# Token rows stored feature block by feature block, and eight expert loads named early

## The chip, the cores and the metric

One core of a Trainium2 chip runs the whole kernel. The number that counts is the device time of one execution, in microseconds (us), from the first to the last instruction plus a small rest around it; the median of several runs is given. Five engines work side by side: TensorE (PE, with its weight loads shown apart as PEld), VectorE (DVE), ScalarE (ACT), GpSimd (POOL) and SyncE (SP), which here issues the DMA transfers.

## The reference, cut to what matters

Two layers of a model work on 256 tokens of 1024 features. The change lies at the border between the Mamba mixer of layer 2 and the mixture of experts that follows it:

```python
def moe_swiglu(h, w_router, w_gate, w_up, w_down):
    t = h.reshape(bsz * seq, d)
    logits = (t @ w_router).astype(jnp.float32)
    top_vals, top_idx = lax.top_k(logits, TOP_K)          # 2 of 8
    top_w = jax.nn.softmax(top_vals, axis=-1)
    gates = jnp.sum(jax.nn.one_hot(top_idx, N_EXPERTS) * top_w[..., None], axis=1)
    out = jnp.zeros_like(t)
    for e in range(N_EXPERTS):
        out = out + gates[:, e:e+1] * swiglu(t, w_gate[e], w_up[e], w_down[e])
```

Each expert has three float32 matrices of 1024 x 2816 (gate, up) and 2816 x 1024 (down), 34.6 MB together.

## The kernel before, in words

**Stages.** Attention, a dense feed-forward, the Mamba mixer and the experts follow each other. The expert stage is more than half of the time: eight experts' weights stream from HBM, each as 33 loads of 1 MB (11 gate, 11 up, 11 down). Line 133 issues the gate and up loads (`load_flat`), line 139 the down loads (`load_rows`), all on SP's queue. They land in tiles named `raw`: eight in one pool, two more in a second pool that opens with the expert stage. `raw()` goes round these ten by the counter `turn`; a load waits until the tile that it will overwrite has been read.

**Experts by rank.** Every expert computes only its own tokens. Experts are sorted by their number of tokens; expert 0 is put first, as rank 0. Ranks 0, 5, 6 and 7 take up to 64 tokens (class `Small`: the weights go to TensorE as they are, lines 1382 and 1401), ranks 1 to 4 up to 128 (class `Expert`: every weight tile is first split into a high and a low part by ACT and DVE at line 159, then multiplied three times, lines 1290 and 1335). The order is rank 0, then 1, 5, then 2, 6, then 3, 4, then 7. These brackets are groups; a group's tokens are fetched together.

**Fetching tokens.** `halves_of` writes the normalised token rows as two tiles, `xt_hi` and `xt_lo` (high and low parts; tokens on the partitions, 1024 features along the row), from four PSUM banks: four ACT instructions (line 1065) and four DVE instructions (line 1066). `gather` then makes, for each of 8 feature blocks `cc`, one PSUM tile by four matmuls (line 1199): a slice of `xt_hi` or `xt_lo` of 128 tokens x 128 features is loaded as weights, and the 0/1 selection tile `psel` streams through (128 columns for one expert, 256 for two). A block `cc` holds the features p*8 + cc, p = 0 to 127, so the slice takes every eighth float of a row. This order fits the weights, whose row p*8 + cc lies on partition p. There are 32 such matmuls in a group and 160 in all. The first group's run before rank 0 starts. Those of the next group are placed by a table of ticks into the down phase of the last expert before it: in ranks 0, 5 and 6 (256 columns each), and in rank 4 (128 columns).

**What sets the order.** The instructions stand on each engine in an order that a scheduler works out at build time from the program; the order in the source is not always kept. `early` holds gate loads of rank 0 that are named inside the last `ssm_out` of the Mamba stage, and `stream` takes them from there. `rankc` (line 1041, 12 KB of constants) and `fn_row` (line 1432, the last norm's gain) are the small loads of the expert stage.

Of the kernel before, what the change touches and what calls it, by code (L numbers as in the profile page):

```python
# [12 lines left out]
F32R = mybir.dt.float32r  # L13
I32 = mybir.dt.int32
U32 = mybir.dt.uint32
AF = mybir.ActivationFunctionType
# [4 lines left out]
P = 128  # L21
S = 256
D = 1024
DC = D // P
# [56 lines left out]
def body(ctx: ExitStack, tc, x, c, positions, ada_w, ada_b, norm_g,  # L81
# [5 lines left out]
    V, A, PE, G, SP = nc.vector, nc.scalar, nc.tensor, nc.gpsimd, nc.sync  # L87
# [10 lines left out]
    def scoped(ectx, name, bufs=1, side="right"):  # L98
        return ectx.enter_context(tc.tile_pool(name=name, bufs=bufs, side=side, reuse_waits="tile"))
# [8 lines left out]
    def pt(tag):  # L108
        pool, tag, n = banks[tag]
        return pool.tile([P, 512], F32, tag=tag, name=tag, bufs=n)  # L110

    extra, turn, halved = [], [0], []

    def raw(n):

        pool = rawp
        if extra:
            pool = rawp if turn[0] < 8 else extra[0]
            turn[0] = (turn[0] + 1) % (8 + NMORE)
        t = pool.tile([P, 2048], F32, tag="raw", name="raw")  # L120
        return t[:, :n]
# [8 lines left out]
    def load_flat(ap, t):  # L130

        d = raw(FLAT)
        SP.dma_start(d, ap.rearrange("(p j) n -> p (j n)", p=P)[:, t * FLAT:(t + 1) * FLAT])
        return d
# [250 lines left out]
    rtok = per.tile([P, 2], F32, name="rtok")  # L385
# [3 lines left out]
    with ExitStack() as lctx:  # L389
# [36 lines left out]
        for q in range(4):  # L426
            ps = pt("mm")
            for i in range(4):
                cc, j = 2 * q + i // 2, i % 2
# [109 lines left out]
        for t in range(8):  # L539
            ps = pt("mm")  # L540
# [3 lines left out]
        for j in range(2):  # L544
            for nh in range(2):
                ps = pt("mm")
# [65 lines left out]
        for half in range(2):  # L612
            w = load8(mla_w_out[0, :, half * 512:(half + 1) * 512])
            for m in range(2):
                ps = pt("mm")
# [77 lines left out]
    early = []  # L693
    with ExitStack() as lctx:
# [36 lines left out]
        ps, psb0 = pt("in"), pt("y")  # L731
# [10 lines left out]
        xb, e, z, w = (four[:, i, :, :] for i in range(4))  # L742
        q = e
# [60 lines left out]
        m = decay_tiles()  # L804
# [113 lines left out]
        for g in range(SG):  # L918
# [31 lines left out]
            m = m2  # L950
# [31 lines left out]
        pst = {}  # L982
# [26 lines left out]

        def then(m):  # L1010
            if m == 2:
                early.append(load_flat(moe_w_gate[0, 0], 0))
            if m:
                finish(m - 1)
            if m == 5:
                logits(0)
            if m == 6:
                token_rows(0)
            if m == 7:
                logits(2)  # L1020
                token_rows(2)
                token_rows(4)
# [13 lines left out]


    extra.append(scoped(ctx, "rawm", NMORE, "left"))
    ep = scoped(ctx, "moe", 1, "left")
    rankc = ep.tile([P, 3, NE], F32, name="rankc")  # L1040
    SP.dma_start(rankc, consts[:, C_KEY:C_EIGHTH].rearrange("p (z e) -> p z e", z=3))
    x_tok = ep.tile([P, 2, D], F32, name="x_tok")
    xt_hi = ep.tile([P, 2, D], F32R, name="xt_hi")
    xt_lo = ep.tile([P, 2, D], F32R, name="xt_lo")

    top = ep.tile([P, 2, 8], F32, name="top")
    tix = ep.tile([P, 2, 8], U32, name="tix")
# [13 lines left out]

    def halves_of(q, j):

        sl, ps = slice(q * 512, (q + 1) * 512), pst[q, j]
        held = A.activation(xt_hi[:, j, sl], ps, AF.Copy, scale=rtok[:, j:j + 1])
        V.scalar_tensor_tensor(xt_lo[:, j, sl], ps, rtok[:, j:j + 1], xt_hi[:, j, sl],
                               op0=ALU.mult, op1=ALU.subtract)
        return held
    with ExitStack() as cctx:
# [4 lines left out]
    ps = pt("y")  # L1074
# [32 lines left out]
    with ExitStack() as cctx:  # L1107
        cctx.enter_context(tc.issue_after(last.ins))
        for j in range(2):
            held = halves_of(1, j)  # L1110
# [81 lines left out]
    def gather(xs, sel2, cc, first=False):  # L1192


        m = len(xs) * P
        ps = pt("a")
        for i in range(4):
            j, src = i // 2, (xt_hi, xt_lo)[i % 2]
            PE.matmul(ps[:, :m], src[:, j, :].rearrange("t (p c) -> t c p", c=DC)[:, cc, :], sel2[:, j, :, :],  # L1199
                      start=(i == 0), stop=(i == 3))  # L1200

        def empty():
            g, sh = gain8[:, 0, cc:cc + 1], gain8[:, 1, cc:cc + 1]
            big = [i for i, x in enumerate(xs) if len(x) == 2]
            for i, x in enumerate(xs):
                if len(x) == 1:
                    A.activation(x[0][:, cc, :], ps[:, i * P:i * P + FEW], AF.Identity, bias=sh, scale=g)
            if not big:
                return
            n = P * (1 + big[-1])  # L1210
            tt = ew.tile([P, 2 * P], F32, tag="gt", name="gt")
            if first:
                V.tensor_scalar(tt[:, :n], ps[:, :n], g, sh, op0=ALU.mult, op1=ALU.add)
            else:
                A.activation(tt[:, :n], ps[:, :n], AF.Identity, bias=sh, scale=g)
            for i in big:
                split(xs[i][0][:, cc, :], xs[i][1][:, cc, :], tt[:, i * P:(i + 1) * P])
        return empty
# [14 lines left out]
    class Expert:  # L1233
# [32 lines left out]
        def stream(self, which):  # L1266

            for t in range(DC * DFF // FLAT):
                w = early.pop() if early else load_flat(self.w[which], t)
                for h in range(2):  # L1270
                    feed(lambda f=t * FLAT + h * HALF, ws=self.take(w[:, h * HALF:(h + 1) * HALF]):
                         self.columns(which, f, ws))
# [167 lines left out]
    for g, i in seq:  # L1440
# [4 lines left out]
        if g:  # L1445
            which = nc.values_load(tid[0:1, rank:rank + 1], engines=[mybir.EngineType.SP], min_val=0, max_val=NE - 1)
# [165 lines left out]
```

## Time and profile before

| | us |
|---|---|
| median of 3 runs (1308.05 to 1312.42) | 1309.12 |
| the profiled execution, its own time | 1308.49 |
| its span, first to last instruction | 1306.2 |
| PE busy | 1261.3 (97%) |
| PE weight loads busy | 1024.8 (78%) |
| DVE busy | 857.7 (66%) |
| ACT busy | 699.9 (54%) |

PE and its weight loads overlap. A matmul's end in the profile is modelled, so a matmul's cost in a row of matmuls is the step from one start to the next, not its duration. "PEclk" is the granted TensorE clock as a share of 2.4 GHz: 0.50 is its lower level, 1.2 GHz. The chain of work that ended last is followed back from the last instruction; times in it are from the span's start.

### The profile page before, as it was taken

Reading aid. Unit: us, or ns where it says so; the run is one execution under the profiler, and the core shown is the slowest. Engines: PE = TensorE matmul, PEld = TensorE weight load, DVE = VectorE, ACT = ScalarE, POOL = GpSimd, SP = SyncE. Lnnn points to the kernel's source line nnn. Section 1 sums busy time; section 2 is a strip of 40 time slices with the busy share of each in tenths; the row PEclk is TensorE's granted clock in tenths of the full one; section 3 lists DMA queues with packets and bytes.
Section 4 is the critical chain, followed back from the end, with each engine's and each line's share of the span. In section 5 each row is a group of like instructions: output and inputs, shape, how many; then the busy total and the mean of one; then the engine's idle time right before and its main releaser. Section 6 shows DMA issues by size and latency. Waiting matters only on the chain.

```text
span 1306.2 us, 21161 instructions
## 1 busy us (share of the span) xinstructions
PE 1261.3 (97%) x8236; PEld 1024.8 (78%) x8236; DVE 857.7 (66%) x1314; ACT 699.9 (54%) x1162; POOL 18.3 (1%) x16
## 2 busy tenths in 40 slices
PE   7999899999999999999999999999999999999996
PEld 6768899999988999996658866488855688888652
DVE  7577787777878888842157860378902789988312
ACT  3568565555568776532247640477603676776302
POOL 4000000000000000000000000000000000000000
PEclk9999999999989999998999999999999999999999
DMA  9885578888932456427999999999999999998895
GB/s 344 312 289 181 194 261 319 322 323 296 323 129 103 156 194 213 175 76 295 420 421 421 383 360 421 421 420 403 342 385 420 420 421 346 376 364 308 301 421 212
DMA packets 104730, 407.96 MB, mean 312 GB/s; under 512 B 10401, under 2 KB 16046, under 8 KB 70958
## 3 DMA queue, kind: packets, MB, share of 16 engines
q1 hardware_dynamic: 104622, 406.53, 81.3%
q8 instruction: 66, 1.08, 0.3%
q14 instruction: 42, 0.34, 0.1%
HBM read 405.46 MB, written 1.05 MB: 311 GB/s over the span
## 4 chain that ended last, share of the span: by engine, by line
PE 86%; DVE 5%; DMA 4%; ACT 3%; issue 1%; SPq 0%; DVEq 0%; ACTq 0%
PE a L1290 18%; PE a L1382 11%; PE y L1335 9%; PE y L1401 4%; PE y L358 3%; PE y L360 3%; PE y L359 3%; PE a L1199 3%; PE gu L358 3%; PE gu L360 3%; PE gu L359 3%; PE in L360 2%; PE in L358 2%; PE in L359 2%; DMA raw<-in_moe_w_down_dram 2%; PE mm L448 2%
## 5 line engine op out<-in xcount | busy, mean ns | idle before, releaser
L159 DVE TENSOR_TENSOR wlo<-raw,whi 128x1024 fp32r<-128x1024 f32 x395 | 466.8, 1218 | 86.4 <-ACT whi L159 85.4
L159 ACT CAST whi<-raw 128x1024 fp32r<-128x1024 f32 x395 | 404.2, 1051 | 187.1 <-PE a L1290 45.2
L1382 PE MATMUL a<-raw,xe 128*64 128x384 f32 (+3 forms) x1280 | 161.2, 412 | 0.0
L1290 PE MATMUL a<-wlo,xe_hi 128*128 128x512 f32 (+1 forms) x464 | 154.3, 346 | 0.3
L1290 PE MATMUL a<-whi,xe_lo 128*128 128x512 f32 (+1 forms) x464 | 153.4, 342 | 0.0
L1382 PEld LDWEIGHTS a<-raw,xe 128*64 128x64 f32 x1280 | 92.0, 135 | 67.7 <-issue 50.9
L1303 DVE TENSOR_TENSOR sg<-sg,a 128x512 f32<-128x512 f32 (+2 forms) x36 | 22.0, 639 | 157.3 <-PE a L1382 145.4
L1290 PE MATMUL a<-whi,xe_hi 128*128 128x256 f32 (+1 forms) x464 | 111.8, 345 | 7.7 <-ACT whi L159 7.7
L220 DVE SCALAR_TENSOR_TENSOR acc<-raw,cond,acc 128x512 f32<-128x512 f32 x140 | 105.5, 766 | 5.7 <-ACT acc L218 4.1
L1290 PEld LDWEIGHTS a<-wlo,xe_hi 128*128 128x128 f32 x464 | 87.9, 189 | 16.3 <-DVE wlo L159 3.6
L358 PE MATMUL gu<-hT_hi,whi 128*128 128x256 f32 x352 | 99.3, 283 | 1.2 <-ACT hT_hi L345 1.2
L359 PE MATMUL gu<-hT_lo,whi 128*128 128x256 f32 x352 | 99.1, 282 | 0.0
L360 PE MATMUL gu<-hT_hi,wlo 128*128 128x256 f32 x352 | 98.8, 281 | 0.0
L1290 PEld LDWEIGHTS a<-whi,xe_lo 128*128 128x128 f32 x464 | 88.1, 190 | 10.1
L1290 PEld LDWEIGHTS a<-whi,xe_hi 128*128 128x128 f32 x464 | 76.3, 189 | 24.1 <-ACT whi L159 14.9
L1401 PE MATMUL y<-raw,at 128*64 128x512 f32 (+1 forms) x364 | 81.4, 586 | 0.8 <-DMA raw<-in_moe_w_down_dram 0.6
L358 PE MATMUL in<-hT_hi,whi 128*128 128x256 f32 (+1 forms) x264 | 76.1, 288 | 0.7 <-DVE r L314 0.7
L360 PE MATMUL in<-hT_hi,wlo 128*128 128x256 f32 (+1 forms) x264 | 75.6, 287 | 0.5 <-DVE wlo L159 0.5
L359 PE MATMUL in<-hT_lo,whi 128*128 128x256 f32 (+1 forms) x264 | 74.7, 283 | 0.0
L358 PEld LDWEIGHTS gu<-hT_hi,whi 128*128 128x128 f32 x352 | 66.8, 190 | 1.5 <-ACT hT_hi L345 1.5
L359 PEld LDWEIGHTS gu<-hT_lo,whi 128*128 128x128 f32 x352 | 67.0, 190 | 0.0
L360 PEld LDWEIGHTS gu<-hT_hi,wlo 128*128 128x128 f32 x352 | 67.0, 190 | 0.0
(399 smaller groups left out, 2321.2 us busy)
## 6 DMA issues: line engine op xcount, KB each, us to landing
raw<-in_moe_w_gate_dram SPq DMA_DIRECT2D x88, 1024.0 KB, 5.9
raw<-in_moe_w_up_dram SPq DMA_DIRECT2D x88, 1024.0 KB, 12.7
raw<-in_moe_w_down_dram SPq DMA_DIRECT2D x85, 1024.0 KB, 11.8
raw<-in_ada_w_dram SPq DMA_DIRECT2D x47, 1024.0 KB, 8.0
raw<-in_ssm_w_in_dram SPq DMA_DIRECT2D x20, 1024.0 KB, 5.2
raw<-in_ffn_w_down_dram SPq DMA_DIRECT2D x11, 1024.0 KB, 8.4
raw<-in_ffn_w_gate_dram SPq DMA_DIRECT2D x10, 1024.0 KB, 8.2
raw<-in_ffn_w_up_dram SPq DMA_DIRECT2D x10, 1024.0 KB, 9.2
```

The source lines that it names most:

```text
L159: return A.copy(hi, src), V.tensor_sub(lo, src, hi)
L220: V.scalar_tensor_tensor(acc, w[k // 4][:, k % 4, :], cond[:, k:k + 1], acc, op0=ALU.mult, op1=ALU.add)
L358: PE.matmul(ps, whi, ahi, start=(first and i == 0), stop=False, skip_group_check=skip)
L359: PE.matmul(ps, whi, alo, start=False, stop=False, skip_group_check=skip)
L360: PE.matmul(ps, wlo, ahi, start=False, stop=(last and i == n - 1), skip_group_check=skip)
L448: PE.matmul(ps, win[k // 3][:, k % 3, sl], h32[:, k, :], start=first and k == 0, stop=k == DC - 1, skip_group_check=True)
L1199: PE.matmul(ps[:, :m], src[:, j, :].rearrange("t (p c) -> t c p", c=DC)[:, cc, :], sel2[:, j, :, :], start=(i == 0), stop=(i == 3))
L1290: PE.matmul(bank[:, o:o + n], a[:, j, :], w[:, m], start=f, stop=l, skip_group_check=True)
L1303: V.tensor_mul(self.sg[:, sl], self.sg[:, sl], self.acc["u", b][:, :n])
L1335: PE.matmul(self.y[b], a, w[:, b * 512:(b + 1) * 512], start=f, stop=l, skip_group_check=True)
L1382: PE.matmul(bank[FEW * h:FEW * (h + 1), o // 2:(o + n) // 2], self.xhi[:, j, :], w[:, h, :], start=first, stop=last, skip_group_check=True)
L1401: res = PE.matmul(self.y[c0 // 512][FEW * h:FEW * (h + 1), c0 % 512:c0 % 512 + n], self.at[t][:, FEW * h:FEW * (h + 1)], ws[h], start=t == ...
```

## The change

It does two things. First, `xt_hi` and `xt_lo` get the shape token x half x block `cc` x p: `halves_of` now reads each PSUM bank with the block outermost (8 runs of 64 floats, each float eight floats from the one before) and writes runs of 64 neighbours, and `gather` loads 128 neighbouring floats as weights where it took every eighth. Second, at tick m == 2 of the last `ssm_out` all eight gate loads 0 to 7 of rank 0 are named instead of load 0 alone, `turn` starts at 8, and `early` is taken from its front.

```diff
             if m == 2:
-                early.append(load_flat(moe_w_gate[0, 0], 0))
+                early.extend(load_flat(moe_w_gate[0, 0], t) for t in range(8))
...
     extra.append(scoped(ctx, "rawm", NMORE, "left"))
+    turn[0] = 8
...
-    xt_hi = ep.tile([P, 2, D], F32R, name="xt_hi")
-    xt_lo = ep.tile([P, 2, D], F32R, name="xt_lo")
+    xt_hi = ep.tile([P, 2, DC, P], F32R, name="xt_hi")
+    xt_lo = ep.tile([P, 2, DC, P], F32R, name="xt_lo")
...
-        sl, ps = slice(q * 512, (q + 1) * 512), pst[q, j]
-        held = A.activation(xt_hi[:, j, sl], ps, AF.Copy, scale=rtok[:, j:j + 1])
-        V.scalar_tensor_tensor(xt_lo[:, j, sl], ps, rtok[:, j:j + 1], xt_hi[:, j, sl],
+        sl, ps = slice(q * 64, (q + 1) * 64), pst[q, j].rearrange("t (p c) -> t c p", c=DC)
+        held = A.activation(xt_hi[:, j, :, sl], ps, AF.Copy, scale=rtok[:, j:j + 1])
+        V.scalar_tensor_tensor(xt_lo[:, j, :, sl], ps, rtok[:, j:j + 1], xt_hi[:, j, :, sl],
                                op0=ALU.mult, op1=ALU.subtract)
...
-            PE.matmul(ps[:, :m], src[:, j, :].rearrange("t (p c) -> t c p", c=DC)[:, cc, :], sel2[:, j, :, :],
+            PE.matmul(ps[:, :m], src[:, j, cc, :], sel2[:, j, :, :],
                       start=(i == 0), stop=(i == 3))
...
-                w = early.pop() if early else load_flat(self.w[which], t)
+                w = early.pop(0) if early else load_flat(self.w[which], t)
```

SP's queue where the expert stage begins, before (lines 1041 and 1432 are the two small loads, `raw_6328` to `raw_6626` are rank 0's gate loads 0 to 7, `raw_6634`, `raw_6644` and `raw_6654` its loads 8, 9 and 10, `raw_6664` up load 0):

```order
L133 DMA raw_6328<-in_moe_w_gate_dram 128x2048
...
L133 DMA raw_6626<-in_moe_w_gate_dram 128x2048
L1041 DMA rankc_6430<-in_consts_dram 128x24
L1432 DMA fn_row_6459<-in_final_norm_dram 128x1024
L133 DMA raw_6644<-in_moe_w_gate_dram 128x2048
L133 DMA raw_6654<-in_moe_w_gate_dram 128x2048
...
L133 DMA raw_6634<-in_moe_w_gate_dram 128x2048
L133 DMA raw_6664<-in_moe_w_up_dram 128x2048
```

The same place after the change (one line lower in the source; `raw_6342` is gate load 7):

```order
L133 DMA raw_6328<-in_moe_w_gate_dram 128x2048
...
L133 DMA raw_6342<-in_moe_w_gate_dram 128x2048
L1042 DMA rankc_6444<-in_consts_dram 128x24
L1433 DMA fn_row_6473<-in_final_norm_dram 128x1024
L133 DMA raw_6634<-in_moe_w_gate_dram 128x2048
L133 DMA raw_6644<-in_moe_w_gate_dram 128x2048
...
L133 DMA raw_6654<-in_moe_w_gate_dram 128x2048
L133 DMA raw_6664<-in_moe_w_up_dram 128x2048
```

Eight gate loads stand ahead of `rankc` in both. Only loads 8, 9 and 10 trade places: load 8 now goes out with load 9, and load 10 is the one that waits for rank 0's first tile.

DVE where the token rows are written, before (`sel` marks each token's experts, `pos` its place in them, `in`, `s` and `y` are PSUM banks):

```order
L1060 TENSOR_TENSOR sel<-m_6438 128x16
L1066 SCALAR_TENSOR_TENSOR xt_lo<-s,rtok,xt_hi 128x512 x2
L1081 TENSOR_TENSOR pos<-y,sel 128x16
L1094 TENSOR_SCALAR psel<-cst,pos 128x128 x2
L1066 SCALAR_TENSOR_TENSOR xt_lo<-in,rtok,xt_hi 128x512
L1066 SCALAR_TENSOR_TENSOR xt_lo<-y,rtok,xt_hi 128x512
```

and after:

```order
L1061 TENSOR_TENSOR sel<-m_6452 128x16
L1067 SCALAR_TENSOR_TENSOR xt_lo<-s,rtok,xt_hi 128x8x64 x2
L1082 TENSOR_TENSOR pos<-y,sel 128x16
L1095 TENSOR_SCALAR psel<-cst,pos 128x128 x2
L1067 SCALAR_TENSOR_TENSOR xt_lo<-in,rtok,xt_hi 128x8x64
L1067 SCALAR_TENSOR_TENSOR xt_lo<-y,rtok,xt_hi 128x8x64
```

The place is the same; the form went from one run of 512 to 8 runs of 64. ACT's four instructions change in the same way, and on PE no instruction moves.

## Rows read from the trace of the kernel before

**Rows 1.** Windows: busy us per engine, PEclk, DMA share, GB/s.
```profile
590.00:592.00 2.00, 2.00 (x10) 1.90 (x9) 1.79 (x12) 1.91 (x3) 0.00 (x0) 0.50 0.99 406
601.00:602.00 1.00, 1.00 (x12) 0.55 (x10) 0.00 (x0) 0.00 (x0) 0.00 (x0) 1.00 0.59 98
670.00:770.00 100.00, 99.00 (x507) 82.45 (x507) 86.47 (x85) 71.68 (x79) 0.00 (x0) 0.98 0.99 399
1248.00:1262.00 14.00, 14.00 (x120) 8.71 (x118) 0.00 (x0) 0.00 (x0) 0.00 (x0) 1.00 1.01 420
```
**Rows 2.** Chain that ended last, in order of time: start us, us, what.
```profile
597.48 41.24 PE a L1382 x313
...
654.25 13.05 PE y L1401 x60
...
842.38 0.76 DVE yg L1347
...
1225.98 21.85 PE a L1382 x168
```
**Rows 3.** Weight loads by shape: busy us, mean ns of one, idle before.
```profile
L1199 PEld LDWEIGHTS a<-psel,xt_lo 128*128 128x128 f32 x80 | 26.8, 336 | 1.3 <-issue 0.8 <-DVE xt_lo L1066 0.3
...
L1249 PEld LDWEIGHTS a<-ej,psel 128*128 128x128 f32 x16 | 2.7, 189 | 2.0 <-ACT xe_hi L159 1.6
```
**Rows 4.** Timeline of PE, gather inside rank 0: start us, us, what.
```profile
644.31 0.40 PE L1199 MATMUL a<-psel,xt_lo 128*128 128x256 f32 x1
644.55 0.41 PE L1249 MATMUL a<-ej,psel 128*128 128x272 f32 x2
644.80 0.39 PE L1199 MATMUL a<-psel,xt_hi 128*128 128x256 f32 x1
```
**Rows 5.** Timeline of PE around the first gather, before rank 0.
```profile
587.59 0.35 PE L1078 MATMUL y<-sel,uones 128*128 128x8 f32 x1
587.80 0.35 PE L1079 MATMUL y<-sel,uones 128*128 128x8 f32 x1
...
593.20 0.44 PE L1199 MATMUL a<-psel,xt_lo 128*128 128x128 f32 x1
...
593.44 0.45 PE L1199 MATMUL a<-psel,xt_hi 128*128 128x128 f32 x1
```
**Rows 6.** Timeline of PE, gather inside rank 4's down phase.
```profile
1199.51 0.23 PE L1199 MATMUL a<-psel,xt_hi 128*128 128x128 f32 x1
...
1200.30 0.67 PE L1335 MATMUL y<-whi,at_hi 128*128 128x512 f32 x2
...
1203.38 0.63 PE L1311 MATMUL a<-cst,sg 128*128 128x128 f32 x4
1203.77 0.42 PE L1199 MATMUL a<-psel,xt_hi 128*128 128x128 f32 x1
...
1204.74 0.68 PE L1335 MATMUL y<-whi,at_hi 128*128 128x512 f32 x2
```
**Rows 7.** Timeline of SP's queue at the start of the expert stage.
```profile
519.41 47.84 SPq L133 DMA_DIRECT2D raw<-in_moe_w_gate_dram  x8
584.79 0.33 SPq L1041 DMA_DIRECT2D rankc<-in_consts_dram  x1
...
585.65 15.45 SPq L133 DMA_DIRECT2D raw<-in_moe_w_gate_dram  x3
```
**Rows 8.** Timeline of SP: last down load of rank 0, of rank 5.
```profile
642.88 0.33 SPq L139 DMA_DIRECT2D raw<-in_moe_w_down_dram  x1
...
815.65 0.33 SPq L139 DMA_DIRECT2D raw<-in_moe_w_down_dram  x1
```
**Rows 9.** DMA issues at 637.5:643.3 and, alike, 810:816: KB, median us to landing.
```profile
raw<-in_moe_w_down_dram SPq DMA_DIRECT2D x3, 1024.0 KB, 19.8
```
**Rows 10.** Lines 1065 and 1066: durations in ns, min/median/max, starts.
```profile
L1065 ACT ACTIVATE xt_hi<-s,rtok x2: 679/683/687, 585.5 to 586.1; 128x512 fp32r<-128x512 f32 x2
...
L1066 DVE SCALAR_TENSOR_TENSOR xt_lo<-s,rtok,xt_hi x2: 743/744/746, 586.8 to 587.4; 128x512 fp32r<-128x512 f32 x2
```

## The prediction

> **What bounds the kernel now.** I read the windows first, for which engine is full in which stretch. In the expert stage PE is busy for 99.00 of 100 us while a 128-token expert runs (670 to 770 us), and at the very end, 1248 to 1262 us, the DMA share is 1.01 at 420 GB/s [rows 1]. So 1,024 KB take 1.05 MB / 420 GB/s = 2.5 us of the transfers, and an expert's 33 loads 82 us. The chain of waits says the same in order of time: it runs along PE through the experts, and leaves PE inside rank 7 at 1225.98 + 21.85 = 1247.8 us, after 168 of its gate and up matmuls, where rank 0 runs 313 in one piece [rows 2]. Rank 7's later loads go out as its tiles are read, so that closing stretch moves as a whole with the time at which rank 7 starts, 1225.98 us [rows 2]. From the end of rank 0 (the DVE step `yg` follows it) to the end of rank 5 it is 842.38 - 667.30 = 175.1 us [rows 2]; the 66 loads of these two experts need 165 us. Transfers therefore have some 10 us to spare in each such pair, and PE time saved there reaches the end as long as no expert catches up with its own loads.
>
> Next the weight loads by shape, since the change touches what they read. Line 1249 and line 1199 both load 128x128 for selection matmuls; the first, whose columns are neighbours, takes 189 ns, the second, which takes every eighth float, 336 ns [rows 3]. What this costs is a step between starts. In the gather inside rank 0 one step of line 1199 is 644.55 - 644.31 = 0.24 us, while two matmuls of line 1249, which stream even more columns (272 against 256), take 644.80 - 644.55 = 0.25 us together, 0.125 each [rows 4].
>
> **The change part by part.**
>
> The eight early loads cost and bring nothing. The queue already sent eight gate loads from 519.41 us on, `rankc` at 584.79 and two more gate loads from 585.65 [rows 7]; the built order of the changed kernel has the same eight ahead of the same two. Loads 8, 9 and 10 trade places, and the load that waits for rank 0's first tile is now load 10, needed later than load 8. No load leaves SP earlier or later. What hides it is that `rankc` and the two loads behind it wait for tile space until the Mamba stage ends; if the queue were reordered after all, 12 KB and 512 KB would move, about 1 us of transfer at 420 GB/s. I take 0.
>
> Writing the rows: ACT's and DVE's four instructions each now read PSUM with steps of eight floats. Contiguous they take 683 and 744 ns [rows 10]. No row of this trace reads PSUM in such steps over hundreds of elements. Bounds: nothing added (the same 512 elements, with writes that stay runs of 64), and what the stepped weight load pays over the contiguous one, 336/189 = 1.78 times [rows 3], so 0.53 us more on each of ACT's four, which stand one behind the other ahead of the first gather: 2.1 us. A gain is excluded, since reads can't get better than neighbours. I take 0, because the one known victim of steps is PE's reader of SBUF, not these engines' reader of PSUM, and keep 2.1 for the range. The Trainium skill speaks against this edit: "Advanced Engine Details and Errata", PSUM Cachelines, says that PSUM lines are 8 bytes (two floats) and that any pattern that isn't contiguous slows matmuls significantly. "VectorE: DVE Perf Modes", Mode 1x (REGULAR), says that the plain mode takes odd strides and PSUM operands at its usual one result a cycle. By the first the cost would lie toward 2.1 us, by the second at 0; no row here settles it.
>
> The first gather (32 matmuls of 128 columns before rank 0) runs at granted clock 0.50, the 1.2 GHz level [rows 1]. Its step is 593.44 - 593.20 = 0.24 us; contiguous weights at the same clock step by 587.80 - 587.59 = 0.21 us, with 8 columns behind them [rows 5]. 31 steps x 0.03 = 0.9 us, all of it on the path: rank 0 starts behind it, and the first transfer after the idle stretch waits for rank 0's first tile.
>
> The gathers inside ranks 0, 5 and 6: 32 matmuls of 256 columns each, at full clock. 32 x (0.24 - 0.125) = 3.7 us of PE for each. They stand between the down matmuls, on PE's own line, so the expert ends 3.7 us earlier unless its last load isn't there yet. That load decides:
> - Rank 0: the last down load is issued at 642.88 and lands 19.8 us later, at 662.7 [rows 8, 9]. PE's 60 down matmuls from 654.25 step by 13.05/60 = 0.2175 us and close the first half of the output at 667.30 [rows 2]; the last load is eight of these matmuls, and four of them lie in that half, so PE takes it up at about 666.4, 3.7 us after it landed. The transfers move up by the 0.9 us of the first gather as well, so PE may come 0.9 + 3.7 = 4.6 us earlier, which is just what it wants (0.9 + 3.7). As the two meet exactly, and rank 1's first loads follow every 2.5 us, I take 4.2 with the 0.9 in it.
> - Rank 5: issued 815.65, lands 835.45 [rows 8, 9]; PE takes it up at 842.38 - 4 x 0.2175 = 841.5 [rows 2], 6.0 us later. Both sides start from the same 4.2 us, so 3.7 fits: I take 3.7.
> - Rank 6 repeats rank 5's pattern: 3.7. In between, ranks 2 and 3 use loads more slowly than they arrive, so transfers catch up with the earlier start.
>
> The gather inside rank 4 streams 128 columns. Where four of its matmuls follow the down matmuls, they take 1200.30 - 1199.51 = 0.79 us, behind transposes 1204.74 - 1203.77 = 0.97 us; four transposes, 128 contiguous columns and as many streamed, take 1203.77 - 1203.38 = 0.39 us [rows 6]. Eight blocks x 0.40 to 0.58 would be 3.2 to 4.6 us; what the longer form has more is the tail of the transposes ahead of it, which stays, so I take 3.3 us. Rank 4 is a 128-token expert and PE sets its time, so it counts in full.
>
> Sum: 4.2 + 3.7 + 3.7 + 3.3 = 14.9 us. Rank 7 then starts 14.9 us earlier and the rest keeps its length. The profiled execution took 1308.49 us, so it would take 1293.6; the median of before stands 0.6 us above that execution, which makes **1294.2 us**.
>
> **The rivals.**
> - *Transfers hold the end of ranks 5 and 6.* If their loads did not follow the earlier start, 3.7 + 3.7 us would turn into waits for the landing of down loads: 1309.1 - 7.5 = 1301.6. For it: the 19.8 us to landing, eight times the 2.5 us of one load. Against it: the 6.0 us of lead, and the 10 us to spare in each pair.
> - *PSUM in steps is dear.* At the upper bound the first gather starts 2.1 us later: 1296.3.
> - *The clock rises earlier.* The granted clock might return to 2.4 GHz part of the way through the first gather, where before it was back only at 601 [rows 1]. Some 20 of its steps at half of 0.21 give 2.0 us, and the half of rank 0's slow 3.5 us from 597.5 [rows 2] gives 1.8 more: 1290.4. Against it: at 0.50 a step shrinks only from 0.24 to 0.21.
> - *The step isn't in the reading.* If line 1199's 0.24 us came from something else than the stepped floats, nothing would change: 1309. Against it: line 1249 reads the same `psel` in the same place at half the step. The Trainium skill's "TensorE: Matmul & The Clock Gate", LDWEIGHTS, counts columns alone, which gives about 107 ns (an estimate from its formula) for both and no gain; 336 against 189 ns [rows 3] does not agree with it.
> - *Slower.* One mechanism: ACT's and DVE's readers of PSUM fall to an eighth of their rate with a step of eight floats. Then each of ACT's four takes 0.68 x 8 = 5.5 us, and rank 0 starts 4 x 4.8 = 19.2 us later; against 14.9 gained that is 1313.4. It decides from 14.9/4 = 3.7 us more per instruction, 6.4 times its present time. Nothing in the trace is that slow for a step.
>
> **How the numbers follow.** Forecast 0.71; transfers hold it 0.10; PSUM dear 0.08; clock 0.04; no gain 0.04; slower 0.03. The time is that of the forecast. The range takes in the clock and the dear PSUM and the bounds of the terms: 1290.0 to 1300.0. It leaves out 0.17. A measurement of this kernel can tell about 0.3% (4 us) from no change: faster 0.71 + 0.10 + 0.08 + 0.04 = 0.93, same 0.04, slower 0.03.
>
> **What the profile after would show.** Weight loads of the gather near 190 ns and steps of 0.12 us at full clock, 0.21 in the first gather. The row-writing ACT and DVE instructions still at 0.68 and 0.74 us (1.2 and 1.3 for the dear case). Rank 0's first matmul near 596.6 instead of 597.5; the ends of ranks 0 and 5 near 663.1 and 834.5; rank 7's start near 1211.1; from there to the end of the span 80 us as before. SP's queue with the same issue times up to 586. The prediction is wrong if PE shows new waits for down loads in ranks 0, 5 or 6 (transfers hold it), if the weight loads stay at 336 ns, or if the first gather starts microseconds late.

## The result

| | before | after |
|---|---|---|
| median, us | 1309.06 (1308.05 to 1312.42, 4 runs) | 1292.02 (1291.23 to 1295.75, 4 runs) |
| the profiled execution | 1308.49 | 1291.27 |
| its span | 1306.2 | 1289.1 |

The ratio is 0.9871, with a 95% interval from 0.9844 to 0.9898: the change is faster by 17.0 us. The forecast was 1294.2, and 14.9 us of gain. The two profiled executions lie 17.2 us apart. The 41 runs of before that were made beside the experiments have a mean of 1308.5, and all 14 runs of after one of 1292.9: 15.6 us. In the three sets of runs that hold both kernels the means lie 16.9, 13.0 and 15.4 us apart. So the terms of the sum have to answer for some 15 us, and the 2 us more between the two profiles are a question of their own (below).

Line numbers of after are one higher than those of before from line 1039 on: the gather is line 1200, gate and up of the 64-token class 1383, its down matmuls 1402, the 128-token class 1291 and 1336.

First the weight loads, answering to [rows 3]: the instructions of line 1200 in the changed kernel (duration in ns as min/median/max, then the first and last start). The maxima are those of the first gather, at the lower clock.

```profile
L1200 PEld LDWEIGHTS a<-psel,xt_hi x80: 186/190/333, 589.1 to 1202.8; 128*128 128x128 f32 x80
L1200 PEld LDWEIGHTS a<-psel,xt_lo x80: 186/189/333, 589.7 to 1202.9; 128*128 128x128 f32 x80
```

From 336 ns they went to 190, the 189 of line 1249 in [rows 3]. The stepped loads of before take the same time at either clock; here are those of the first gather (clock 0.50) and those inside rank 0 (clock 1.00):

```profile
L1199 PEld LDWEIGHTS a<-psel,xt_hi x15: 334/338/340, 589.8 to 596.7; 128*128 128x128 f32 x15
...
L1199 PEld LDWEIGHTS a<-psel,xt_hi x15: 312/338/344, 639.9 to 653.5; 128*128 128x128 f32 x15
```

The steps between starts follow. The timeline of PE inside rank 0 (256 columns, answering to [rows 4]), and in the first gather at clock 0.50 (answering to [rows 5]); start us, us, what:

```profile
642.20 0.28 PE L1200 MATMUL a<-psel,xt_lo 128*128 128x256 f32 x1
642.32 0.27 PE L1200 MATMUL a<-psel,xt_hi 128*128 128x256 f32 x1
642.43 0.28 PE L1200 MATMUL a<-psel,xt_lo 128*128 128x256 f32 x1
```
```profile
593.18 0.41 PE L1200 MATMUL a<-psel,xt_hi 128*128 128x128 f32 x1
593.40 0.41 PE L1200 MATMUL a<-psel,xt_lo 128*128 128x128 f32 x1
593.61 0.41 PE L1200 MATMUL a<-psel,xt_hi 128*128 128x128 f32 x1
```

0.12 us for 0.24, and 0.21 for 0.24. In rank 4 (128 columns, answering to [rows 6]) four matmuls behind the down matmuls take 1185.46 - 1185.07 = 0.39 us, where they took 0.79:

```profile
1185.07 0.22 PE L1200 MATMUL a<-psel,xt_hi 128*128 128x128 f32 x1
...
1185.24 0.28 PE L1200 MATMUL a<-psel,xt_hi 128*128 128x128 f32 x1
1185.35 0.27 PE L1200 MATMUL a<-psel,xt_lo 128*128 128x128 f32 x1
1185.46 0.68 PE L1336 MATMUL y<-whi,at_hi 128*128 128x512 f32 x2
```

The chain of waits of after, in order of time (answering to [rows 2]; start us, us, what):

```profile
596.80 41.63 PE a L1383 x317
...
642.51 19.84 DMA raw<-in_moe_w_down_dram
662.39 1.10 PE y L1402 x4
663.52 0.76 DVE yg L1348
...
833.48 0.76 DVE yg L1348
...
1208.88 36.31 PE a L1383 x288
1245.21 19.91 DMA raw<-in_moe_w_down_dram
```

Rank 0 starts 0.7 us earlier and ends 3.8 us earlier (`yg` at 663.52 against 667.32). In this execution its end hangs on a transfer: PE idles 0.18 us for the last down load, which stands in the chain (timeline of PE, with the idle time in brackets):

```profile
662.39 1.94 PE L1402 MATMUL y<-raw,at 128*64 128x512 f32 x8 [0.18 <-DMA raw<-in_moe_w_down_dram]
```

In the two repeats of after (below) PE does not wait there, and the chain runs through the 60 down matmuls. Rank 5 ends 8.9 us earlier (842.38 to 833.48), rank 7 starts 17.1 us earlier (1225.98 to 1208.88), and from there to the end of the span it is 80.2 us, as it was.

The edits that were to cost nothing: the row-writing instructions, which now read PSUM in steps of eight floats (lines 1066 and 1067, answering to [rows 10]), and SP's queue (answering to [rows 7]):

```profile
L1066 ACT ACTIVATE xt_hi<-s,rtok x2: 681/684/687, 585.6 to 586.2; 128x512 fp32r<-128x512 f32 x2
...
L1067 DVE SCALAR_TENSOR_TENSOR xt_lo<-s,rtok,xt_hi x2: 741/742/744, 586.9 to 587.5; 128x512 fp32r<-128x512 f32 x2
```
```profile
519.51 47.84 SPq L133 DMA_DIRECT2D raw<-in_moe_w_gate_dram  x8
584.89 0.33 SPq L1042 DMA_DIRECT2D rankc<-in_consts_dram  x1
...
585.74 15.04 SPq L133 DMA_DIRECT2D raw<-in_moe_w_gate_dram  x3
```

684 and 742 ns against 683 and 744; the same issues, their starts within 0.1 us. The third of the last line, which waits for rank 0's first tile, goes out 0.3 us earlier than before.

### The profile page after: what moved, and what is told of

The parts are those of the page before. It is cut to its first block, busy times and chain, and to the rows that moved or that the text cites. A ratio compares the mean times of both kernels' runs of the same rounds, so it can differ in the third digit from the quotient of the medians.

```text
span 1289.1 us, 21161 instructions
## 1 busy us (share of the span) xinstructions
PE 1244.1 (97%) x8236; PEld 1006.7 (78%) x8236; DVE 857.4 (67%) x1314; ACT 698.4 (54%) x1162; POOL 18.3 (1%) x16
## 4 chain that ended last, share of the span: by engine, by line
PE 86%; DMA 4%; DVE 4%; ACT 3%; issue 2%; SPq 0%; ACTq 0%; DVEq 0%
PE a L1291 18%; PE a L1383 12%; PE y L1336 10%; DMA raw<-in_moe_w_down_dram 4%; PE y L1402 3%; PE y L358 3%; PE gu L358 3%; PE gu L359 3%; PE gu L360 3%; PE y L359 3%; PE y L360 3%; PE in L360 2%; PE in L358 2%; PE in L359 2%; PE mm L448 2%
## 5 line engine op out<-in xcount | busy, mean ns | idle before, releaser
L1291 PEld LDWEIGHTS a<-whi,xe_hi 128*128 128x128 f32 x464 | 75.9, 188 | 24.0 <-ACT whi L159 14.9
```

Of the source, the lines that this page charges most:

```text
L1291: PE.matmul(bank[:, o:o + n], a[:, j, :], w[:, m], start=f, stop=l, skip_group_check=True)
```

## The stretches, as measured in every profile

The start of the expert stage alone wanders by 7 us from one execution to the next (583.7 to 591.0 us), so ends are compared by stretches. "Rank 0" runs here from ACT's first row-writing instruction to the `yg` of rank 0 and takes in the first gather; "rank 5" from its first gate matmul to its `yg`; "rank 4" from its first gate matmul to rank 7's. "Falls" are returns of the granted clock to 0.50 for 3.4 us where a 128-token expert follows a 64-token one (three such handovers). Times in us, each from the trace of one execution. For before and after, the first gate matmuls of ranks 5 and 4 follow; the `yg` of rank 5 stands in the chains, and rank 7's first gate matmul starts at 1225.91 and 1208.81:

```profile
771.38 1.12 PE L1382 MATMUL a<-raw,xe 128*64 128x512 f32 x4
...
1119.91 0.63 PE L1290 MATMUL a<-whi,xe_hi 128*128 128x512 f32 x2
```
```profile
766.31 1.12 PE L1383 MATMUL a<-raw,xe 128*64 128x512 f32 x4
...
1106.14 0.63 PE L1291 MATMUL a<-whi,xe_hi 128*128 128x512 f32 x2
```

| kernel | rank 0 | rank 5 | rank 6 | rank 4 | falls |
|---|---|---|---|---|---|
| before | 81.80 | 71.00 | 71.00 | 106.00 | 2 |
| before_again | 81.75 | 71.00 | 71.00 | 106.01 | 2 |
| loads_alone | 81.79 | 71.01 | 71.00 | 106.02 | 2 |
| after | 77.90 | 67.17 | 67.17 | 102.67 | 0 |
| after_again | 77.68 | 67.17 | 67.16 | 102.68 | 0 |
| after_third | 77.52 | 67.16 | 67.16 | 102.67 | 0 |
| layout_alone | 77.84 | 67.16 | 67.17 | 102.68 | 3 |
| stepped_in_first | 77.93 | 67.17 | 67.17 | 102.69 | 0 |
| stepped_in_rank0 | 81.71 | 67.17 | 67.16 | 102.67 | 3 |
| stepped_in_rank56 | 77.75 | 71.00 | 71.00 | 102.68 | 0 |
| stepped_in_rank4 | 77.34 | 67.17 | 67.17 | 106.01 | 1 |

## The experiments

Diffs are against the changed kernel; ratios against before in the same set of runs.

**Each half alone.** `layout_alone` takes the loads back, `loads_alone` the layout.

```diff
-                early.extend(load_flat(moe_w_gate[0, 0], t) for t in range(8))
+                early.append(load_flat(moe_w_gate[0, 0], 0))
...
-    turn[0] = 8
...
-                w = early.pop(0) if early else load_flat(self.w[which], t)
+                w = early.pop() if early else load_flat(self.w[which], t)
```

> The changed kernel without the early naming of eight loads: the block layout of the token rows alone. Theory (the whole gain is the contiguous weight loads of the gathers): the same as the full change, 1292 us within 2 us, 17 us under the kernel before. Rival (the early loads bring part of it): slower than the full change by what they bring, at most the 12 us for which the transfers idle between 588 and 601 us.

Measured: 1292.25 (1287.51 to 1294.11, 4 runs), ratio 0.9871, 0.9833 to 0.9909.

```diff
-    xt_hi = ep.tile([P, 2, DC, P], F32R, name="xt_hi")
+    xt_hi = ep.tile([P, 2, D], F32R, name="xt_hi")
...
-        held = A.activation(xt_hi[:, j, :, sl], ps, AF.Copy, scale=rtok[:, j:j + 1])
+        held = A.activation(xt_hi[:, j, sl], ps, AF.Copy, scale=rtok[:, j:j + 1])
...
-            PE.matmul(ps[:, :m], src[:, j, cc, :], sel2[:, j, :, :],
+            PE.matmul(ps[:, :m], src[:, j, :].rearrange("t (p c) -> t c p", c=DC)[:, cc, :], sel2[:, j, :, :],
```

> The kernel before with the early naming of eight loads alone, token rows in their old order. Theory (the queue order was already so): 1309 us within 2 us, the eight gate loads at the same times up to 567 us, rankc at 585. Rival: faster by some us, with rank 0's gate loads landing earlier.

Measured: 1307.75 (1305.12 to 1310.42, 10 runs), ratio 0.9994, 0.9979 to 1.0009. Its weight loads (lines grouped by shape: busy us, mean ns of one, idle before) are those of before:

```profile
L1200 PEld LDWEIGHTS a<-psel,xt_lo 128*128 128x128 f32 x80 | 26.8, 336 | 1.3 <-issue 0.8 <-DVE xt_lo L1067 0.3
```

The layout brings all of the gain; of the loads none shows, in the ratio or in any stretch of the table.

**One gather at a time.** Four kernels give the stepped reading back to one group of matmuls; `g` counts the gathers (0 before rank 0, 1 inside rank 0, 2 and 3 inside ranks 5 and 6, 4 inside rank 4; the lines that hand it on are left out here). The group then fetches other features, with the same amount of work.

```diff
-            PE.matmul(ps[:, :m], src[:, j, cc, :], sel2[:, j, :, :],
+            rows = src[:, j, cc, :]
+            if g == 1:
+                rows = src[:, j, :, :].rearrange("t c p -> t (c p)").rearrange("t (p c) -> t c p", c=DC)[:, cc, :]
+            PE.matmul(ps[:, :m], rows, sel2[:, j, :, :],
```

> The changed kernel, but the 32 weight loads of the gather inside rank 0 take every eighth float again (of the new tile, so they fetch other features: the data of ranks 1 and 5 are wrong, the work is the same). Theory (PE's 3.7 us there are on the path, and in the changed kernel rank 0's end waits for its last load): slower than the full change by 3.1 us, the end of rank 0 then being set by PE again, 0.6 less than the 3.7 us that PE loses; rank 1 starts at 670.8 us instead of 667.7. Rival (transfers alone set the end of rank 0): no change, 1292.

Measured: 1295.54 (1293.88 to 1299.1, 4 runs), ratio 0.9901, 0.9869 to 0.9933. The chain of this kernel at the end of rank 0 (start us, us, what) has no transfer in it; PE runs through its down matmuls to the end, as in [rows 2]:

```profile
654.90 13.05 PE y L1405 x60
667.98 0.76 DVE yg L1351
```

Rank 0 takes 81.71 us for 77.7: its own gather is worth 4.0 us in this one trace, where I expected 3.1, and the contiguous kernels spread from 77.3 to 77.9. With all else contiguous the transfers alone bring nothing. That no transfer stands in the chain doesn't set this kernel apart, since the repeats of after have none either; the length does.

> The changed kernel, but the weight loads of the two gathers inside ranks 5 and 6 take every eighth float again (of the new tile, so the data of ranks 2, 3, 4 and 6 are wrong, the work is the same). Theory (both on the path in full): slower than the full change by 2 x 3.8 = 7.6 us, the stretch from rank 5's first matmul to its last output 70.9 us instead of 67.1. Rival (transfers hold the ends of these ranks): by less than 2 us.

Measured: 1297.9 (1296.54 to 1299.25, 5 runs), ratio 0.9925, 0.9901 to 0.9950. Each of the two stretches is 3.83 us longer and nothing else moved, so the two gathers are worth 7.7 us; the median, 5.9 us above that of after, says the same within its spread.

> The changed kernel, with the 32 gather matmuls inside rank 4 alone (128 columns each) reading every eighth float as weights again; that group then fetches the wrong features (rank 7's tokens), and the amount of work stays the same. Theory (PE paces rank 4, so each of its eight blocks counts in full): from rank 4's first gate matmul to rank 7's first it takes 106.0 us instead of 102.7, rank 7 starts 3.3 us later, the time is 3.3 us above the changed kernel's, about 1295.3. Rival (half of the blocks hide behind the conversion of the weights): 1.6 us, about 1293.6. Ranks 0, 5 and 6 stay at 67 us each.

Measured: 1296.3 (1293.56 to 1299.29, 4 runs), ratio 0.9918, 0.9893 to 0.9944. Rank 4 takes 106.01 us for 102.67: 3.34 us. All eight blocks count in full; the rival, with half of them hidden, would have been 1.6. The block that took 0.39 us in after takes 0.79 here (timeline of PE):

```profile
1201.12 0.23 PE L1203 MATMUL a<-psel,xt_hi 128*128 128x128 f32 x1
1201.19 0.40 PE L1203 MATMUL a<-psel,xt_lo 128*128 128x128 f32 x1
...
1201.91 0.68 PE L1339 MATMUL y<-whi,at_hi 128*128 128x512 f32 x2
```

> The changed kernel, with the 32 matmuls of the first gather, before rank 0, reading every eighth float as weights again; rank 0 then gets the wrong features, and the amount of work stays the same. What it tells: whether the 0.7 us by which rank 0 started earlier is worth 0.7 to 0.9 us at the end, as forecast, or less. Theory now: rank 0's first matmul comes 0.7 us later, near 597.5, but the granted clock comes back to 1.00 at the same 600 to 601 us, so that less of rank 0 runs at 0.50, and the first transfer after the pause is issued 0.3 to 0.4 us later: the end of rank 0 is 0.3 to 0.4 us later, near 663.9, and the time is 0.3 us above the changed kernel's. By the prediction's term it would be 0.9 us. No difference of medians can tell these apart; the stretches of the profile can.

Measured: 1295.44 (1292.86 to 1297.57, 4 runs), ratio 0.9910, 0.9886 to 0.9934; the median can't tell a term of this size, as said ahead. From the first row-writing instruction to rank 0's first matmul it is 11.87 us, where the contiguous kernels have 11.11. To the end of rank 0 it is 77.93 against 77.34 to 77.90 in six of them (after and its repeats, `layout_alone`, `stepped_in_rank56`, `stepped_in_rank4`; mean 77.67). Of the 0.76 us at the start some 0.3 is left at the end, within the spread of those six. With rank 0's own gather stepped it is 0.07 (81.78, the mean of the three kernels stepped throughout, to 81.71 in `stepped_in_rank0`). The granted clock shows where it goes: it comes back to 1.00 2.8 us after rank 0's first matmul in this kernel and 3.2 to 3.7 us after it in the contiguous ones, so what starts earlier runs longer at half speed.

**The same kernels again.** The first profiles had 2 falls of the clock in before, none in after, and three in `layout_alone`, whose instructions stand in the order of after.

> The changed kernel as it is. What it tells: whether the fall of the granted clock to 0.50 for some 3.4 us, where a 128-token expert follows a 64-token one, belongs to the order of the work or to the single execution. In the changed kernel's first profile it fell at none of the three handovers, in the kernel with the row layout alone, whose instructions stand in the same order, at all three. Theory (it is the single execution's): one to three falls here, each making the stretch of its 128-token expert 1.0 to 1.3 us longer (101.3 to 101.7 instead of 100.3 us). Rival (something in the changed kernel prevents it): none again. Ranks 0, 5 and 6 take 66.8 and 67.2 us and rank 4 102.7 in either case. The median stays at 1291 to 1293.

Measured: 1294.56 (1293.97 to 1296.12, 4 runs), ratio 0.9896, 0.9873 to 0.9919. No fall, and a median 1.6 us above the 1291 to 1293 that I expected; the profiled execution reached the expert stage 5.2 us later than the first one of after.

> The changed kernel as it is, a third time, beside the kernel with the pauses filled. Theory: the 64-token experts take 66.6 and 67.2 us and rank 4 102.7 as in the two executions before; from the first row-writing instruction of ACT to the end of rank 0 it takes 77.3 to 77.9 us; the time at which that instruction starts (585.6 and 590.8 us in the first two) and the number of falls of the clock at the three handovers (0 and 0) are the execution's own, so either may differ; median 1291 to 1295.

Measured: 1291.94 (1288.05 to 1294.46, 6 runs), ratio 0.9885, 0.9865 to 0.9905.

> The kernel before as it is, a second profile. Theory (the falls of the clock at the handovers are the execution's own): 0 to 3 falls, not bound to the 2 of the first profile; ranks 0, 5 and 6 take 69.9 and 71.0 us and rank 4 106.0 as in the first. Rival (the layout of before brings the falls about): 2 again.

Measured: 1311.91, one run. The windows (busy us and count per engine, PEclk, DMA share, GB/s) around rank 0's handover in before_again, then in after:

```profile
670.00:672.00 2.00, 0.74 (x4) 0.00 (x0) 1.32 (x2) 1.28 (x2) 0.00 (x0) 1.00 1.01 422
672.00:674.00 2.00, 1.45 (x4) 0.59 (x4) 1.90 (x4) 2.00 (x4) 0.00 (x0) 1.00 1.00 418
674.40:677.80 3.40, 3.40 (x9) 2.64 (x8) 3.40 (x4) 2.42 (x4) 0.00 (x0) 0.50 1.01 419
```
```profile
664.00:666.00 2.00, 0.38 (x3) 0.05 (x1) 1.21 (x3) 1.69 (x3) 0.00 (x0) 1.00 1.00 418
666.00:669.40 3.40, 3.13 (x10) 1.71 (x11) 3.40 (x5) 3.35 (x4) 0.00 (x0) 1.00 1.01 422
```

In both PE idles 1.6 us and then 0.2 us until ACT has converted the first weights of rank 1 (at 672.34 in before_again, at 665.96 in after). Then in the one the clock is at 0.50 (the 1.2 GHz level) for 3.4 us, from 2 us after PE took up work again, and in the other not. A fall makes its 128-token expert 1.0 to 1.3 us longer: rank 1 takes 101.66, 101.64 and 101.68 us with one, 100.33 to 100.46 without. My expectation, that the falls are the single execution's luck, does not hold: all three profiles with the stepped layout throughout (before, its repeat, `loads_alone`) have them at the same two handovers, and all three of after have none. Nor is the layout what decides, since `layout_alone` has three.

What separates the profiles at the first handover is a time. In the four whose rank 0 has the stepped gather, `yg` comes 67.0 to 67.2 us after the clock's return inside rank 0, and all four have a fall; in nine with the shorter rank 0 it comes 62.9 to 63.4 us after it, and none has one; in `layout_alone` it comes 63.6 us after it, with a fall (the three kernels below are among the nine, though with their pause filled). The third handover separates likewise: in `stepped_in_rank4`, `yg` of rank 6 comes 402.84 us after the clock's return, with a fall, and in after, its repeats and `stepped_in_first` 403.05 to 403.22 us after it, without (`stepped_in_rank56`, at 410.9 us, has none either). PE's pause is the same in all of them. That is a correlation. It fits that shortening rank 0 moves the pause to where the clock mostly stays; in `layout_alone` PE waited 0.35 us for rank 0's last load, which put its `yg` later. No run moved the pause alone.

**PE kept busy.** Three kernels fill PE's pauses with matmuls whose result is not used. `gap_filled` puts 12 behind the last down matmul of ranks 0, 5 and 6:

```diff
+            if b and t == DFF // (2 * P) - 1:
+                ps = pt("a")
+                for _ in range(12):
+                    PE.matmul(ps[:, :P], w[:, D + 512:D + 512 + P], ones, start=True, stop=True)
```

> The changed kernel, with 12 more matmuls of 128 columns behind the last down matmul of each of ranks 0, 5 and 6, on the last down tile and a constant; their result is not used. They stand in the 1.6 us in which PE waits for the first converted weights of the next expert. What it tells: whether the pause of PE is what precedes the fall of the granted clock at these handovers. Theory: with the pause filled the clock stays at 1.00 at all three handovers, the 128-token experts behind them take 100.3 us each, and the median is up to 2 us under the changed kernel's, 1289 to 1292. Rivals: the clock falls there all the same in one to three of them (the pause is not what matters), median as the changed kernel's; or the dummies hold back the first real matmuls and the load that waits for the last down tile, 12 x 0.125 = 1.5 us in each of three ranks at most, which gives 1293 to 1296.

Measured: 1290.06 (1288.94 to 1292.61, 4 runs), ratio 0.9867, 0.9842 to 0.9893. No fall at the handovers. As after's repeats have none either, this doesn't show that the filling keeps the clock. Each filling matmul took 0.22 us, not 0.125 (the trace has two instructions for each, 24 for the 12), so PE took up the next expert 1.0 us later; that expert ended no later (99.4 us for 100.4), so the first microsecond of PE's work there is not what it waits for.

`pauses_filled` adds 21 ahead of the matmuls that count the tokens, before the first gather:

```diff
+    with ExitStack() as cctx:
+        cctx.enter_context(tc.issue_after(chosen.ins))
+        for _ in range(21):
+            PE.matmul(ps[:, P:2 * P], ones, ones, start=True, stop=True)
```

> The kernel with the pauses at the handovers filled, and 21 more matmuls of 128 columns of a constant ahead of the five that count the tokens, in the 2.6 us in which PE waits for the choice of experts before the first gather; their result is not used. What it tells: whether the half clock from 586.8 to 600.4 us, through the first gather and the first 3.4 us of rank 0, follows from PE's pause before it, and what it costs. Theory (it does): the clock stays at 1.00 or falls later and for less, 31 steps of the first gather shrink from 0.21 to 0.125 us (2.6 us) and rank 0's first 3.5 us by half (1.7 us); from the first row-writing ACT instruction to rank 0's start it takes 8.5 us instead of 11.1, to rank 0's end 73.4 instead of 77.7 if the transfers follow, which leave their own pause as soon as rank 0's first tile is read. The median is then some 4 us under that of the changed kernel. Rival (the clock falls all the same): 11.1 and 77.7 us as before, no gain, and up to 0.5 us lost where the dummies stand ahead of the counting. Second rival (the transfers don't follow): PE waits at the end of rank 0 for its last down load, gain 2 to 3 us.

Measured: 1289.50 (1288.64 to 1294.25, 4 runs), ratio 0.9863, 0.9843 to 0.9884. Windows of this kernel through the filling, the wait for the token rows, the first steps of the gather, and the fall:

```profile
585.83:592.40 6.57, 6.57 (x60) 6.51 (x59) 2.96 (x15) 4.52 (x11) 0.00 (x0) 1.00 0.32 112
592.40:594.90 2.50, 1.14 (x7) 0.85 (x7) 2.32 (x9) 0.97 (x2) 0.00 (x0) 1.00 1.01 426
594.90:596.06 1.16, 1.16 (x12) 1.16 (x12) 1.05 (x7) 1.14 (x2) 0.00 (x0) 1.00 1.02 431
596.06:602.89 6.83, 6.83 (x26) 4.48 (x27) 3.47 (x21) 4.41 (x12) 0.00 (x0) 0.50 0.12 52
```

With the pause filled the clock stays at 1.00 into the gather, is low for 6.8 us instead of 13.7, and the steps before the fall are 0.11 us. But 21 matmuls of 0.22 us are longer than the pause, the counting starts 1.6 us late, and rank 0 starts after 10.90 us instead of 11.11. It ends after 77.40 us, not the 73.4 that I expected: the last down load, with PE waiting 0.12 us for it, is in the chain again, as the second rival has it. The median lies 2.4 us under that of after_third, beside which it ran, where I expected some 4. `pauses_sized` has 13 there and 7 at the handovers.

> The kernel with the pauses filled, with the filling sized by what one such matmul was seen to take (0.22 us, not 0.125): 13 ahead of the five that count the tokens instead of 21, and 7 at each handover instead of 12; their results are not used. What it tells: whether the filling pays once it holds nothing back. Theory: the five counting matmuls start when the choice of experts is there, 1.4 us after the first row-writing instruction of ACT; the first gather runs its first matmuls at 0.11 us a step, and the clock falls to 0.50 later than it did (in the kernel with the pauses filled at 596.1, 2.9 us into the gather) and comes back after a shorter time. From the first row-writing instruction to rank 0's first matmul it takes 8.1 to 9.5 us instead of 11.1, to the end of rank 0 74 to 76.5 instead of 77.5; no fall at the handovers; the median is 1 to 3 us under the changed kernel's, 1287 to 1290. Rival (nothing to be had, because the clock falls for 13.65 us all the same): 11.1 and 77.5 us, median 1291 to 1294.

Measured: 1293.8 (1289.74 to 1296.25, 5 runs), ratio 0.9861, 0.9838 to 0.9884. Windows of the wait for the rows and the fall:

```profile
592.96:594.62 1.66, 0.34 (x3) 0.24 (x2) 1.62 (x6) 1.41 (x3) 0.00 (x0) 1.00 1.01 252
594.62:604.86 10.24, 10.03 (x40) 7.75 (x41) 5.78 (x32) 6.74 (x14) 0.00 (x0) 0.50 0.45 188
```

A wait of some 1.5 us remains between the counting and the gather, and this time the clock fell as the gather began, for 10.2 us. Rank 0 starts after 11.02 us and ends after 77.01, 0.7 us less than the mean of after's three. Most of what I expected (8.1 to 9.5, and 74 to 76.5) isn't there. The ratios of the three filled kernels, 0.9861 to 0.9867, lie below those of after, 0.9871 to 0.9896, but the intervals overlap: a version that beats after is not shown. In one set the four runs of `gap_filled` (1288.9 to 1292.6) all lie below the four of after_again (1294.0 to 1296.1), but the stretch that the filling could change, from rank 0's `yg` to rank 5's first matmul, is 102.8 us in `gap_filled` as in after; of the 6.3 us between the two profiled executions, 5.7 lie ahead of the expert stage.

## Why the prediction was right

| step | forecast, us | measured, us | from |
|---|---|---|---|
| early loads | 0 | 0 | `loads_alone`, ratio 0.9994 |
| writing the rows | 0 (bound +2.1) | 0 | 684 and 742 ns |
| rank 0, with the first gather | 4.2 | 4.1 | 81.78 to 77.70, means of three |
| ... its first gather alone | 0.9 | 0.76 at the start, 0.1 to 0.3 at the end | `stepped_in_first`, `stepped_in_rank0` |
| rank 5, rank 6 | 3.7 each | 3.83 each | 71.00 to 67.17 |
| rank 4 | 3.3 | 3.33 | 106.00 to 102.67 |
| rank 7 to the end | 0 | 0 | 80.2 in both |
| sum | 14.9 | 15.1 | |
| falls of the clock | not thought of | 2.3 | ranks 1 and 2 of the first two profiles |

- **The mechanism.** A weight load of every eighth float costs 336 ns and one of neighbours 190. PE's step goes with it, by less than the loads differ, because they overlap in the trace: 0.24 and 0.12 us at full clock. At clock 0.50 the stepped load still takes 338 ns and steps by 0.24, while one of neighbours takes 333 and steps by 0.21, so there the layout brings little. Line 1249 in [rows 3] and [rows 4] gave the price in advance, and the term of ranks 5 and 6 was short by 0.13 us only because the step came to 0.12 where I had put 0.125. The rival that the step isn't in the reading falls with the first view of after, and with it the Trainium skill's "TensorE: Matmul & The Clock Gate", LDWEIGHTS, where it counts columns alone: 336 and 190 ns are loads of the same 128 columns.
- **Rank 0.** The prediction had PE's wish (4.6 us) and the transfers' meeting, and took 4.2; 4.1 was measured. The transfers moved up by 0.4 us (the last down load is issued at 642.51 for 642.88) and not by 0.9. In the first profile of after PE waits 0.18 us for that load. This is the new wait that the prediction named as a sign against it, but it is small, and the two repeats don't have it. Two parts inside the term were mis-sized. The first gather is worth 0.1 to 0.3 us at the end and not 0.9: in all the traces of the table the clock comes back 14.3 to 14.8 us after the first row-writing instruction, whichever way the first gather reads, so a rank 0 that starts earlier runs longer at half clock. And rank 0's own gather is not cut: it brings 3.9 to 4.0 us (81.78 to 77.93, 81.71 to 77.67). The two errors cancel, which is luck.
- **Ranks 5 and 6.** The rival that transfers hold their ends is out: both stretches shrink by the whole 3.83 us, as the 6.0 us of lead said.
- **PSUM in steps.** The upper bound of 2.1 us did not come: the readers take 684 and 742 ns. The warning of the Trainium skill's "Advanced Engine Details and Errata", PSUM Cachelines, is written of matmuls; carried over to ACT and DVE reading 512 floats in steps of 32 bytes, as the prediction did for its bound, it does not hold. For DVE, the plain mode in the Trainium skill's "VectorE: DVE Perf Modes", Mode 1x (REGULAR), agrees.
- **The clock rival** gave 1290.4 by an earlier return of the clock in the first gather. The clock did not return earlier (600.2 before, where the prediction read 601 off a window, and 600.4 after), so this rival did not happen, though the time came near it.
- **What was missed.** 14.9 us was the forecast and the profiles lie 17.1 apart at rank 7's start: rank 0 -3.9, ranks 5 and 6 -3.8 each, rank 4 -3.3, ranks 1 and 2 -1.3 and -1.0 for falls of the clock that after does not have, and a start of the stage 0.1 later. Rank 5's end came at 833.48, 1.0 us ahead of the forecast 834.5, for the first of these falls. Over all runs the gain is 15.6 us, so on the average less than 2.3 us of that comes in. It stays open how much of it belongs to the change: the first profiles and their repeats say 2 falls against none, `layout_alone` says three.

## What to carry to other kernels

Where PE's weights are read in steps, compare in the trace a weight load of the same size whose columns are neighbours, at the same granted clock: the difference between the steps from start to start, times the count of loads, is the gain from storing them in the order in which they are read, if the place is one where PE sets the end. The difference between the loads' own durations says too much (here 146 ns for 0.12 us a step). Look for the storing side's price too; here ACT and DVE took the steps, reading PSUM, at no cost. And count in stretches between two landmarks of the program rather than in absolute times: where the clock keeps its level they repeat to a few hundredths of a microsecond, and a whole run wanders by several.

## What the runs showed of the hardware that I had not expected

- **Runs differ by the granted clock.** Of before's 41 runs the shortest has 1303.36 us and the longest 1313.97; the mean granted clock and the time go together (correlation -0.84). The stretches of ranks 4 to 6 repeat to 0.03 us between executions; rank 0, with a change of level in it, spreads over 0.6 us. In two executions of after the expert stage starts at 585.6 and 590.8 us, with 31 and 41 us at clock 0.50 ahead of it; over all 14 traces it starts at 583.7 to 585.6 us with 27 or 31 us of it, at 585.5 to 588.2 with 34 or 38, and at 588.8 to 591.0 with 41.
- **A pause of PE of 1.6 us, and 0.2 more, can be followed by 3.4 us at half clock or by none**, in the same place of the program, at 1.0 to 1.3 us a fall.
- **Busy matmuls ahead of the first gather shortened its half clock and did not remove it**, in one execution each: 13.7 us low without filling, 6.8 in `pauses_filled` and 10.2 in `pauses_sized`. In `pauses_filled` the clock fell while PE was at work, after 1.2 us without a pause, ahead of which PE had idled for 1.4 us of 2.5.
- **A stepped weight load takes no notice of TensorE's clock**: 338 ns at 0.50 and at 1.00, with 0.24 us a step at both. A load of neighbours takes 333 and 190 ns, with 0.21 and 0.12 us a step, so at half clock the layout is worth 0.03 us a step and at full clock 0.12.
- **Steps of 32 bytes cost TensorE's weight load 1.77 times (336 to 190 ns) and cost ACT's and DVE's reading of PSUM nothing** (684 and 742 ns to 683 and 744).
